# First projection of an attention and FFN layer in blocks of 2, 4 and 10 k-tiles, with moved transposes and another allocation order

## The chip, the cores and the metric

One core of a Trainium2 chip runs the whole layer as one program. The metric is the time of one execution in device microseconds (us), as the median of three runs: 2285.63 us for the kernel before. The profile is of one further execution on the same program.

## The reference

The reference is one encoder layer on x of 512 tokens by 2048 features in float32. Cut to what matters here:

```python
mod = c_act @ w_ada[l] + b_ada[l]                       # 2048 x 12288 weights for one vector
sh1, sc1, gt1, sh2, sc2, gt2 = split(mod, 6)
h = rms_norm(x, g_norm1[l]) * (1 + sc1) + sh1
proj = h @ w_in[l]                                      # q, k, v of 8 differential heads, latents
a_out = differential_attention(q_d, k_d, v_d, lam, rel_bias)
b_out = latent_attention(q_m, k_m, v_m)                 # 8 heads from the latents
x = x + gt1 * (concatenate([a_out, b_out]) @ w_out[l])
h2 = rms_norm(x, g_norm2[l]) * (1 + sc2) + sh2
x = x + gt2 * ((silu(h2 @ w_gate[l]) * (h2 @ w_up[l])) @ w_down[l])
```

## The kernel before

Every product is made of three matmuls on operands that are split into a high and a low part (`mm3`, lines 241 to 243): high by high, high by low, low by high. ACT makes the high part of a weight chunk (line 89), DVE or POOL the low part (line 97). PE runs its instructions in the order of the program; the instructions of the other engines are put in order by a scheduler, which follows the program's order loosely.

**First stage.** x is held as 16 tiles `xs[t][b]` of 128 x 512. The modulation's shift and scale for `nk` k-tiles of 128 features are sums over 16 rows of w_ada per partition: `ada_pair` loads 512 KB a step into one of five `araw` buffers (line 330) and DVE adds it, times c, to an accumulator (lines 334 and 336). `ada_columns` turns a finished accumulator into columns with small matmuls (line 347). `modulation` scales x by rstd, transposes each k-tile on PE (line 398), and ACT and DVE make from it the high and low parts `hh` and `hl` (lines 400 to 402). One k-tile of one head is 12 matmuls of 384 columns.

The k-tiles come in the blocks (0, 2), (2, 2), (4, 4), (8, 4), (12, 4), given as first tile and count. For each block the first five heads (`FIRST = 5`) run `head_block`, and the partial result goes to SBUF (`raw_in`; line 506 copies, line 508 adds). In the last block only head 0 runs there; the last four tiles of heads 1 to 4 are the first part of the filling. While a block runs, `run` steps two generators as PE's estimated progress goes on: the sums for the block after next, and the modulation of the next block. What is left of them is emptied at the block's end. Ahead of the first block stand the loads in the order of `LOADS` (`a` a step of the sums, `x` a tile of x, `w` the first weight chunk).

**Attention.** `projections` is one long generator of matmuls: the rest of heads 1 to 4, all 16 k-tiles of heads 5 to 7, the latents (`cq`, `ckv`, `latents`), then four pairs of latent heads and parts of the output projection. `Filler` runs so many us of it, by its own prices, at each F of a written order of steps: s scores, t transposes of probabilities, v values, n norm of the next head, o its operands, e `finish` of the head before. `finish` transposes on PE four tiles `z`, the last of which POOL scales at the end of the head before (lines 739 to 742, 748). `fill.until` runs the generator in one piece until a condition holds. Behind the first pair the generator yields nothing until the latent heads start.

**FFN.** Gate and up run first plainly for two column groups, then in units of seven block products with operands `comb` and `wh`, `wl` (lines 1253 to 1255). The down projection runs in six parts over the hidden features with the same `project` as the output projection. Its stationary tiles are `ax` (part 0: `act0`), its moving tiles the weights `hi` and `lo` of pool `fw`. In the program before, pool `fd` holds per partition 16 tiles `sums` of 2048 bytes, `gt2` of 8192 bytes, `pad` of 32 bytes, then 32 tiles `ax` of 2048 bytes and four `x1r`. `ax` starts at byte 126,944 of a partition, the weights `hi` of the down projection at 44,480. In the output projection the stationary `mh` tiles start at 108,512 and multiples of 2048 behind it, the moving `hi` at 212,960. In the units the moving `comb` starts at 85,984, the stationary `wh` at 44,480.

Of the kernel before, what the change touches and what calls it, by code (L numbers as in the profile page):

```python
# [18 lines left out]
P = 128  # L19
# [18 lines left out]
FIRST = 5  # L38
NEAR = 0.2
LOADS = "aaaxxxxaxxxxaxxxxaxxxxwaa"  # L40
BLOCKS = ((0, 2), (2, 2), (4, 4), (8, 4), (12, 4))
# [157 lines left out]
def hybrid_layer(ctx, tc, a, out):  # L199
# [182 lines left out]
    sums1 = {k0: [] for k0, _ in BLOCKS}  # L382

    def modulation_sums(k0, nk):
        yield from ada_pair(raws0, accs0, 1, 0, k0, nk, sums1[k0])

    def modulation(k0, nk):
        for b in range(1, 4):
            if k0 <= 4 * b - 2 < k0 + nk:
                with tc.issue_after(last_hh[0]):  # L390
                    for t in range(NT):
                        act.activation(xs[t][b], xs[t][b], AF.Copy, scale=rstd1[:, t:t + 1])
        ada_columns(sums1[k0], k0, nk, G1, SH1, C_G1, C_BSC1, C_BSH1)
        yield None
        for kc in range(k0, k0 + nk):
            ps = bank(spare[0], "ps_x")
            for t in range(NT):
                pe.transpose(ps[:, tsl(t)], xs[t][kc // 4][:, tsl(kc % 4)], ident)
            xt, hh, hl = slot("xt", F32), slot("hh"), slot("hl")
            act.activation(xt, ps, AF.Identity, scale=G1[:, kc:kc + 1], bias=SH1[:, kc:kc + 1])  # L400
            last_hh[0] = act.copy(out=hh, in_=xt).ins
            dve.tensor_tensor(out=hl, in0=xt, in1=f(hh), op=ALU.subtract)  # L402
            hT[kc] = (hh, hl)
            yield None

    first = modulation_sums(*BLOCKS[0])
    i = 0
    for kind in LOADS:
        if kind == "a":
            next(first)  # L410
        elif kind == "w":
            W.split(0)
        else:
            t, b = divmod(i, 4)
            sp.dma_start(out=xs[t][b], in_=x[t * P:(t + 1) * P, b * 512:(b + 1) * 512])
            i += 1
# [39 lines left out]
    for t in range(NT):  # L456
        if t % 2:
            act.activation(xs[t][0], xs[t][0], AF.Copy, scale=rstd1[:, t:t + 1])
        else:
            dve.tensor_scalar(out=xs[t][0], in0=xs[t][0], scalar1=rstd1[:, t:t + 1], scalar2=None, op0=ALU.mult)  # L460

# [85 lines left out]
    for gen in (first, modulation(*BLOCKS[0]), modulation_sums(*BLOCKS[1])):  # L547
        for _ in gen:
            pass
    def run(gen, total, at, start, end):  # L550

        n = total * min(1.0, max(0.0, (at - start) / (end - start)))
        while gen[1] < n:
            gen[1] += 1
            next(gen[0], None)

    for i, (k0, nk) in enumerate(BLOCKS):
        final = i + 1 == len(BLOCKS)
        ahead = [modulation_sums(*BLOCKS[i + 2]) if i + 2 < len(BLOCKS) else iter(()), 0]
        near = [iter(()) if final else modulation(*BLOCKS[i + 1]), 0]  # L560
        heads = range(1 if final else FIRST)
        for h in heads:
            tag = next_tag()
            spare[0] = "tmp" if tag == "acc" else "acc"
            for j, _ in enumerate(head_block(h, k0, nk, tag)):
                at = (h + j / nk) / len(heads)
                run(ahead, 16, at, 0.0, 0.9)
                run(near, 7, at, NEAR, 0.95)
        for gen in (ahead[0], near[0]):
            for _ in gen:  # L570
                pass
# [818 lines left out]
    side = gate2()  # L1390
    pads.append(fd[1].tile([P, 8], F32, name="pad"))
# [3 lines left out]
    for i, n in enumerate(PARTS):  # L1395
        for b in range(4):
# [4 lines left out]
            if b == 0 and i + 1 < n_parts:  # L1401
# [40 lines left out]
DIFF_STEPS = "s0 F e s1 n F t0 F s2 v0 F t1 F s3 v1 F t2 F o0 v2 t3 F o1 v3 F"  # L1442
# [45 lines left out]
```

## Time and profile before

| | before |
|---|---|
| median of three runs | 2285.63 us (2285.3 to 2287.18) |
| the profiled execution | 2284.71 us |
| its span in the profile | 2282.9 us |
| mean granted clock | 0.989 |
| PE busy | 2194.7 us of the span |
| DVE busy | 1646.3 us of the span |
| DMA | 344.99 MB, mean 151 GB/s |

The span runs from the first to the last instruction. A busy PE isn't a PE at its peak: matmuls overlap in the records, so the distance between their starts tells the rate. A granted clock of 1.00 is 2.4 GHz, of 0.5 it is 1.2 GHz, and numbers between are means over a stretch.

### The profile page before, as it was taken

The numbers are of one execution on the slowest core, as the hardware profiler recorded it, in microseconds if no ns is written. First come the engines' busy times: TensorE is split into PE (matmuls) and PEld (weight loads), VectorE is DVE, ScalarE is ACT, GpSimd is POOL, SyncE is SP. The second block draws the span as 40 slices with busy tenths as digits, with TensorE's granted clock in tenths as the row PEclk, the third lists the DMA queues.
The fourth block names the chain that finished last, engine by engine and source line by source line (L and its number), as shares of the span: only waits on it lengthen the run. The fifth ranks groups of instructions, "written<-read, shape, count | busy, mean of one in ns | idle before, by whom it ended". The sixth has DMA issues, their size and how long they took to land.

```text
span 2282.9 us, 35317 instructions
## 1 busy us (share of the span) xinstructions
PE 2194.7 (96%) x13878; PEld 2004.6 (88%) x13878; DVE 1646.3 (72%) x2360; ACT 945.1 (41%) x1569; POOL 263.0 (12%) x408
## 2 busy tenths in 40 slices
PE   3899999998989999999999999999999999999999
PEld 2799989997778787899999999999999888888887
DVE  5987787868988686857777777777777676343654
ACT  4423555557555334534444444444444522221221
POOL 0002533436544000000000000000000000000000
PEclk9999999999999999999999999999999999999999
DMA  9975355432433685423333333333333786332442
GB/s 297 322 233 145 90 155 157 131 92 88 162 120 121 214 283 186 135 83 124 121 130 121 121 130 110 122 121 121 112 129 121 253 282 202 101 121 92 157 139 101
DMA packets 270825, 344.99 MB, mean 151 GB/s; under 512 B 15005, under 2 KB 171142, under 8 KB 270530
## 3 DMA queue, kind: packets, MB, share of 16 engines
q1 hardware_dynamic: 267864, 338.18, 45.8%
q10 hardware_dynamic: 2794, 4.55, 0.6%
q8 instruction: 108, 1.77, 0.3%
q14 instruction: 59, 0.48, 0.1%
HBM read 322.71 MB, written 19.96 MB: 150 GB/s over the span
## 4 chain that ended last, share of the span: by engine, by line
PE 68%; DVE 3%; DMA 2%; issue 1%; ACT 0%; POOL 0%; SPq 0%; DVEq 0%; ACTq 0%; POOLq 0%
PE ps_d L243 7%; PE ps_d L242 7%; PE ps_d L241 7%; PE ps_X L1253 5%; PE ps_X L1254 5%; PE ps_X L1255 5%; PE ps_W L1253 3%; PE ps_W L1255 3%; PE ps_W L1254 3%; PE ps_o L241 2%; PE ps_o L243 2%; PE ps_o L242 2%; PE ps_Y L1255 2%; PE ps_Z L1255 2%; PE ps_Z L1253 2%; PE ps_Y L1253 2%
## 5 line engine op out<-in xcount | busy, mean ns | idle before, releaser
L89 ACT CAST hi<-raw 128x1024 fp32r<-128x1024 f32 (+2 forms) x228 | 221.2, 971 | 508.2 <-PE ps_d L242 303.1
L97 DVE TENSOR_TENSOR lo<-raw,hi 128x1024 fp32r<-128x1024 f32 (+2 forms) x215 | 242.7, 1130 | 234.3 <-ACT hi L89 232.4
L1236 ACT CAST wh<-wr 128x1024 fp32r<-128x1024 f32 x160 | 168.6, 1054 | 242.5 <-PE ps_X L1254 68.2
L1254 PE MATMUL ps_X<-comb,wh 128*128 128x256 f32 x960 | 267.9, 279 | 0.0
L1253 PE MATMUL ps_X<-comb,wh 128*128 128x256 f32 x960 | 267.9, 279 | 0.0
L1255 PE MATMUL ps_X<-comb,wl 128*128 128x256 f32 x960 | 267.9, 279 | 0.0
L241 PE MATMUL ps_d<-hi,ax 128*128 128x512 f32 x640 | 253.1, 396 | 0.0
L242 PE MATMUL ps_d<-hi,ax 128*128 128x512 f32 x640 | 253.1, 395 | 0.0
L243 PE MATMUL ps_d<-lo,ax 128*128 128x512 f32 x640 | 253.1, 395 | 0.0
L1219 DVE TENSOR_TENSOR wl<-wr,wh 128x1024 fp32r<-128x1024 f32 x160 | 195.7, 1223 | 73.6 <-ACT wh L1236 73.5
L243 PE MATMUL ps_in<-lo,hh 128*128 128x384 f32 (+2 forms) x704 | 233.1, 331 | 9.8 <-DVE lo L97 9.8
L241 PE MATMUL ps_in<-hi,hh 128*128 128x384 f32 (+2 forms) x704 | 237.9, 338 | 3.4 <-ACT hi L89 2.6
L242 PE MATMUL ps_in<-hi,hl 128*128 128x384 f32 (+2 forms) x704 | 232.3, 330 | 0.8 <-DVE hl L402 0.7
L1236 ACT CAST wh<-wt 128x1024 fp32r<-128x1024 f32 x120 | 126.2, 1051 | 195.6 <-PE ps_X L1254 118.8
L1219 DVE TENSOR_TENSOR wl<-wt,wh 128x1024 fp32r<-128x1024 f32 x120 | 146.8, 1224 | 78.5 <-ACT wh L1236 78.5
L1254 PEld LDWEIGHTS ps_X<-comb,wh 128*128 128x128 f32 x960 | 180.4, 188 | 0.0
L1253 PEld LDWEIGHTS ps_X<-comb,wh 128*128 128x128 f32 x960 | 180.4, 188 | 0.0
L1255 PEld LDWEIGHTS ps_X<-comb,wl 128*128 128x128 f32 x960 | 180.4, 188 | 0.0
L1253 PE MATMUL ps_W<-comb,wh 128*128 128x256 f32 x640 | 179.2, 280 | 0.9 <-DVE cu L1264 0.9
L1254 PE MATMUL ps_W<-comb,wh 128*128 128x256 f32 x640 | 178.6, 279 | 0.0
L1255 PE MATMUL ps_W<-comb,wl 128*128 128x256 f32 x640 | 178.6, 279 | 0.0
L243 PEld LDWEIGHTS ps_in<-lo,hh 128*128 128x128 f32 x704 | 136.5, 194 | 11.4 <-DVE lo L97 11.4
(320 smaller groups left out, 5328.1 us busy)
## 6 DMA issues: line engine op xcount, KB each, us to landing
raw<-in_w_down_dram SPq DMA_DIRECT2D x88, 512.0 KB
araw<-in_w_ada_dram SPq DMA_DIRECT2D x80, 512.0 KB
wr<-in_w_gate_dram SPq DMA_DIRECT2D x40, 1024.0 KB
wr<-in_w_up_dram SPq DMA_DIRECT2D x40, 1024.0 KB
ada<-in_w_ada_dram SPq DMA_DIRECT2D x128, 256.0 KB
raw<-in_w_in_dram SPq DMA_DIRECT2D x128, 192.0 KB
raw<-in_w_out_dram SPq DMA_DIRECT2D x32, 512.0 KB
x<-in_w_ada_dram SPq DMA_DIRECT2D x64, 256.0 KB
```

The source lines that it names most:

```text
L89: nc.scalar.copy(out=hi[:, :n], in_=raw[:, :n])
L97: e.tensor_tensor(out=lo[:, :n], in0=raw[:, :n], in1=hi[:, :n].bitcast(F32), op=ALU.subtract)
L241: pe.matmul(o, ah, bh, start=start, stop=False)
L242: pe.matmul(o, al, bh, start=False, stop=False)
L243: pe.matmul(o, ah, bl, start=False, stop=stop)
L1219: dve.tensor_tensor(out=out, in0=x, in1=y, op=ALU.subtract)
L1236: act.copy(out=hi, in_=src)
L1253: pe.matmul(ps[bk], wh[:, k], c[:, 0], start=first and k == 0, stop=False, skip_group_check=True)
L1254: pe.matmul(ps[bk], wh[:, k], c[:, 1], start=False, stop=False, skip_group_check=True)
L1255: pe.matmul(ps[bk], wl[:, k], c[:, 0], start=False, stop=k == 7, skip_group_check=True)
```

## The change

The words that come with it: first stage in blocks of 2, 4 and 10 k-tiles with six heads, x loaded first; five heads' last ten k-tiles as filling; also pad order and later transposes. `FIRST` is not touched by the diff.

x is loaded ahead of all else. The first two k-tiles get their sums, transposes and evacuation before any head. The sums and modulations of the other k-tiles are paced by windows of PE's estimated us (`MODULATE`), and at a block's end those that start below the end of the next block are emptied. In the step order of the differential heads `e` moves back by two fillings. In the down projection the first tile pair of part 1 is loaded ahead of the allocation of `pad`. A scratch area of SBUF gets 1024 bytes per partition; before, it had 16,384.

```diff
+MODULATE = ((0, 2, (0, 0), (0, 0)), (2, 4, (0.0, 21.0), (21.0, 25.0)), (6, 4, (23.0, 40.0), (41.0, 48.0)),
+            (10, 4, (40.0, 58.0), (59.0, 66.0)), (14, 2, (58.0, 67.0), (67.5, 74.0)))
-BLOCKS = ((0, 2), (2, 2), (4, 4), (8, 4), (12, 4))
+BLOCKS = ((0, 2), (2, 4), (6, 10))
...
+    def evacuate(kc, ps, both):
+        xt, hh, hl = slot("xt", F32), slot("hh"), slot("hl")
+        if both:
+            last_hh[0] = act.activation(hh, ps, AF.Identity, scale=G1[:, kc:kc + 1], bias=SH1[:, kc:kc + 1]).ins
+            dve.tensor_scalar(out=xt, in0=ps, scalar1=G1[:, kc:kc + 1], scalar2=SH1[:, kc:kc + 1], op0=ALU.mult,
+                              op1=ALU.add)
+        else:
+            act.activation(xt, ps, AF.Identity, scale=G1[:, kc:kc + 1], bias=SH1[:, kc:kc + 1])
+            last_hh[0] = act.copy(out=hh, in_=xt).ins
+        dve.tensor_tensor(out=hl, in0=xt, in1=f(hh), op=ALU.subtract)
+        hT[kc] = (hh, hl)
...
+    for i in range(16):
+        t, b = divmod(i, 4)
+        sp.dma_start(out=xs[t][b], in_=x[t * P:(t + 1) * P, b * 512:(b + 1) * 512])
...
+    k0, nk, _, _ = MODULATE[0]
+    for _ in modulation_sums(k0, nk):
+        pass
+    spare[0] = "acc"
+    psx = [turned(kc) for kc in range(k0, k0 + nk)]
+    spare[0] = "tmp"
+    W.split(0)
+    W.load(1)
+    W.load(2)
+    ada_columns(sums1[k0], k0, nk, G1, SH1, C_G1, C_BSC1, C_BSH1)
+    for i in range(nk):
+        evacuate(k0 + i, psx[i], True)
+    W.split(1)
...
+    def run(g, at):
+        gen, n, done, (start, end) = g
+        due = n * min(1.0, max(0.0, (at - start) / (end - start)))
+        while g[2] < due:
+            g[2] += 1
+            next(gen, None)
+
+    at = 0.0
+    side1 = [[paced(modulation_sums(k0, nk), 4 * nk + 1, s), paced(modulation(k0, nk), nk + 1, m)]
+             for k0, nk, s, m in MODULATE[1:]]
     for i, (k0, nk) in enumerate(BLOCKS):
         final = i + 1 == len(BLOCKS)
+        for h in range(1 if final else FIRST):
             tag = next_tag()
             spare[0] = "tmp" if tag == "acc" else "acc"
+            for us in head_block(h, k0, nk, tag):
+                for pair in side1:
+                    for g in pair:
+                        run(g, at)
+                at += us * 1.07
+        while not final and side1 and MODULATE[-len(side1)][0] < BLOCKS[i + 1][0] + BLOCKS[i + 1][1]:
+            for g in side1.pop(0):
+                for _ in g[0]:
+                    pass
         if i == 1:
             load_small()
...
     side = gate2()
+    more = load_acts(1)
+    next(more)
     pads.append(fd[1].tile([P, 8], F32, name="pad"))
...
-            if b == 0 and i + 1 < n_parts:
+            if b == 0 and 0 < i < n_parts - 1:
                 more = load_acts(i + 1)
...
-DIFF_STEPS = "s0 F e s1 n F t0 F s2 v0 F t1 F s3 v1 F t2 F o0 v2 t3 F o1 v3 F"
+DIFF_STEPS = "s0 F s1 n F t0 F e s2 v0 F t1 F s3 v1 F t2 F o0 v2 t3 F o1 v3 F"
...
-    nc = _bacc.Bacc("TRN2", target_bir_lowering=False, num_devices=1)
+    nc = _bacc.Bacc("TRN2", target_bir_lowering=False, num_devices=1, dynamic_dma_scratch_size=1024)
```

## Rows read from the trace of the kernel before

**Rows 1.** The page, first part: busy us, share of the span, instructions of each engine.

```profile
PE 2194.7 (96%) x13878; PEld 2004.6 (88%) x13878; DVE 1646.3 (72%) x2360; ACT 945.1 (41%) x1569; POOL 263.0 (12%) x408
```

**Rows 2.** Windows: length, then busy us (instructions) by engine; granted clock, DMA share, GB/s.

```profile
core 0: us, PE busy (x) PEld busy (x) DVE busy (x) ACT busy (x) POOL busy (x), PEclk, DMA share, GB/s
33.00:157.70 124.70, 107.09 (x565) 103.11 (x566) 114.42 (x150) 49.52 (x78) 0.00 (x0) 0.93 0.95 304
0.00:20.00 20.00, 0.31 (x1) 0.18 (x1) 6.24 (x12) 6.85 (x15) 0.20 (x4) 1.00 0.76 237
20.00:40.00 20.00, 3.27 (x16) 3.27 (x16) 9.50 (x18) 9.95 (x26) 1.21 (x2) 1.00 1.08 353
100.00:120.00 20.00, 13.80 (x54) 13.49 (x55) 19.46 (x25) 4.96 (x7) 0.00 (x0) 0.74 0.93 302
```

**Rows 3.** PE: one group up to 215.4 us; timeline starts: 50 matmuls, and the stage's last.

```profile
L241 PE MATMUL ps_in<-hi,hh 128*128 128x384 f32 x256 | 91.8, 359 | 3.2 <-ACT hi L89 2.6 <-ACT hh L401 0.7
...
199.84 0.33 PE L241 MATMUL ps_in<-hi,hh 128*128 128x384 f32 x1
...
208.33 0.33 PE L242 MATMUL ps_in<-hi,hl 128*128 128x384 f32 x1
...
215.26 0.33 PE L243 MATMUL ps_in<-lo,hh 128*128 128x384 f32 x1
```

**Rows 4.** Timeline of PE up to the first head's first matmul: start, length, instructions.

```profile
36.73 1.87 PE L347 MATMUL ps_ada<-ones,adaacc 128*128 128x1 f32 x8 [32.14 <-DVE adaacc L336]
38.46 1.95 PE L398 MATMUL ps_x<-ident,xs 128*128 128x128 f32 x8
41.07 0.69 PE L241 MATMUL ps_in<-hi,hh 128*128 128x384 f32 x1 [0.66 <-ACT hh L401]
```

**Rows 5.** DVE groups up to 200 us (busy us, mean ns, idle before); timeline: the last sum.

```profile
L336 DVE SCALAR_TENSOR_TENSOR adaacc<-araw,c_col,adaacc 128x1024 f32<-128x1024 f32 x45 | 57.6, 1279 | 0.4 <-DMA araw<-in_w_ada_dram 0.2
L97 DVE TENSOR_TENSOR lo<-raw,hi 128x768 fp32r<-128x768 f32 x30 | 28.5, 954 | 10.3 <-ACT hi L89 9.7
L508 DVE TENSOR_TENSOR raw_in<-raw_in,ps_in 128x384 f32<-128x384 f32 x48 | 25.7, 549 | 4.8 <-PE ps_in L243 4.7
L336 DVE SCALAR_TENSOR_TENSOR adaacc<-araw,c_col,adaacc 128x512 f32<-128x512 f32 x30 | 22.5, 751 | 12.5 <-DMA araw<-in_w_ada_dram 11.7
L402 DVE TENSOR_TENSOR hl<-xt,hh 128x512 fp32r<-128x512 f32 x16 | 11.0, 687 | 2.4 <-ACT hh L401 2.3
...
156.38 1.27 DVE L336 SCALAR_TENSOR_TENSOR adaacc<-araw,c_col,adaacc 128x1024 f32<-128x1024 f32 x1
```

**Rows 6.** DMA issues up to 210 us: count and KB each.

```profile
araw<-in_w_ada_dram SPq DMA_DIRECT2D x48, 512.0 KB
...
araw<-in_w_ada_dram SPq DMA_DIRECT2D x32, 256.0 KB
xs<-in_x_dram SPq DMA_DIRECT2D x16, 256.0 KB
```

**Rows 7.** PE's waits, 217 to 520 us (us, times, longest); a window as in rows 2.

```profile
PE ps_zT L748 <- POOL z L742: 9.3, 4, 5.6
...
320.00:340.00 20.00, 14.41 (x74) 13.40 (x74) 13.08 (x31) 6.39 (x14) 9.34 (x13) 0.91 0.46 130
```

**Rows 8.** Windows around the change from differential to latent heads.

```profile
510.00:530.00 20.00, 17.72 (x113) 15.77 (x112) 12.17 (x24) 17.62 (x60) 11.61 (x32) 0.91 0.26 84
540.00:570.00 30.00, 24.99 (x140) 21.67 (x139) 26.47 (x65) 18.55 (x51) 19.56 (x39) 0.94 0.33 115
```

**Rows 9.** Timeline of PE, first and last of 51 (down), 52 (out), 51 (units) matmuls.

```profile
1999.92 0.40 PE L242 MATMUL ps_d<-hi,ax 128*128 128x512 f32 x1
...
2011.58 0.40 PE L241 MATMUL ps_d<-hi,ax 128*128 128x512 f32 x1
...
783.62 0.39 PE L242 MATMUL ps_o<-hi,ml 128*128 128x512 f32 x1
...
795.18 0.39 PE L242 MATMUL ps_o<-hi,ml 128*128 128x512 f32 x1
...
1059.76 0.28 PE L1255 MATMUL ps_Z<-comb,wl 128*128 128x256 f32 x1
...
1065.60 0.28 PE L1254 MATMUL ps_W<-comb,wh 128*128 128x256 f32 x1
```

More of the change, by code (lines that the diff above doesn't have):

```diff
@@ L38 @@
 FIRST = 5
-NEAR = 0.2
-LOADS = "aaaxxxxaxxxxaxxxxaxxxxwaa"
-BLOCKS = ((0, 2), (2, 2), (4, 4), (8, 4), (12, 4))
+MODULATE = ((0, 2, (0, 0), (0, 0)), (2, 4, (0.0, 21.0), (21.0, 25.0)), (6, 4, (23.0, 40.0), (41.0, 48.0)),
+            (10, 4, (40.0, 58.0), (59.0, 66.0)), (14, 2, (58.0, 67.0), (67.5, 74.0)))
+BLOCKS = ((0, 2), (2, 4), (6, 10))
 PARTS = (2, 4, 4, 4, 4, 4)
@@ L381, in hybrid_layer, with turned @@
     last_hh = [None]
-    sums1 = {k0: [] for k0, _ in BLOCKS}
+    sums1 = {m[0]: [] for m in MODULATE}
     def modulation_sums(k0, nk):
         yield from ada_pair(raws0, accs0, 1, 0, k0, nk, sums1[k0])
+    def evacuate(kc, ps, both):
[9 more added lines that the diff above has]
+        hT[kc] = (hh, hl)
+    def turned(kc):
+        ps = bank(spare[0], "ps_x")
+        for t in range(NT):
+            pe.transpose(ps[:, tsl(t)], xs[t][kc // 4][:, tsl(kc % 4)], ident)
+        return ps
     def modulation(k0, nk):
@@ L395, in modulation @@
         for kc in range(k0, k0 + nk):
[L396 to L403, printed above, removed]
-            yield None
[L406 to L416, printed above, removed]
+            evacuate(kc, turned(kc), False)
+            yield None
+    for i in range(16):
+        t, b = divmod(i, 4)
+        sp.dma_start(out=xs[t][b], in_=x[t * P:(t + 1) * P, b * 512:(b + 1) * 512])
     ps = bank("tmp", "ps_small")
@@ L545, in bias_strips, with paced @@
             sp.dma_start(out=vecd[:, i * 512:(i + 1) * 512], in_=vec[0:H, :])
[L547 to L555, printed above, removed]
+    def paced(gen, n, span):
+        return [gen, n, 0, span]
+    def run(g, at):
[7 more added lines that the diff above has]
+             for k0, nk, s, m in MODULATE[1:]]
     for i, (k0, nk) in enumerate(BLOCKS):
         final = i + 1 == len(BLOCKS)
[L559 to L562, printed above, removed]
+        for h in range(1 if final else FIRST):
             tag = next_tag()
             spare[0] = "tmp" if tag == "acc" else "acc"
[L565 to L571, printed above, removed]
+            for us in head_block(h, k0, nk, tag):
[7 more added lines that the diff above has]
+                    pass
         if i == 1:
```

## The prediction

> **What bounds the kernel now.** I read the page first: PE is busy 2194.7 of 2282.9 us [rows 1], so nearly all that can be won lies where PE waits, and in how far apart its matmuls start. Windows show where it waits. Until the first matmul of a head at 41.07 us it does almost nothing [rows 4], and from there to 120 us it runs in pieces, with a granted clock of 0.74 between 100 and 120 us [rows 2]; that is a part of the time at 1.2 instead of 2.4 GHz. At full clock the 384-column matmuls of this stage start 8.49 us / 49 = 0.1733 us apart [rows 3]. The 3 x 256 of them up to head 0's last block [rows 3] are 768 x 0.1733 = 133.1 us of work, and the last one starts at 215.3 us [rows 3]: some 82 us of this stage went elsewhere, 41 of them before the first matmul.
>
> What PE waits for there is DVE's sums of w_ada. From 33 us to 157.7 us, where the last sum begins at 156.38 us [rows 5], DVE is busy 114.42 of 124.70 us, while the DMA share is 0.95 at 304 GB/s [rows 2]. DVE is the nearer bound and DMA close behind. After that PE is full, but for two kinds of holes: 9.3 us of waits of the transposes of finish() for POOL's z, the longest 5.6 us [rows 7], and the change from the differential heads to the latent heads, where PE is busy 17.72 of 20 us and 24.99 of 30 us [rows 8].
>
> The last view is the timeline of steady stretches. In the down projection 512-column matmuls start 11.66 us / 50 = 0.2332 us apart; in the output projection, which is the same function with the same shapes, 11.56 us / 51 = 0.2267 us; in the gate and up units 256-column ones 5.84 us / 50 = 0.1168 us [rows 9]. Nothing waits in any of them.
>
> **The change, part by part.** I sum against the profiled execution's 2284.7 us; the median is 0.9 us above it.
>
> *First stage.* The words speak of six heads and of five as filling; the diff leaves FIRST at 5, so five heads run blocks 0 and 1, head 0 alone runs the ten-tile block, and four heads' ten tiles become filling. PE's work up to head 0's last block falls from 64 to 5 x 6 + 10 = 40 head-tiles of 12 matmuls, 480 x 0.1733 = 83.2 us; the other 49.9 us go into the filling, which between 217 and 520 us loses only the waits of [rows 7], so they count there at full rate. The first stage gains if head 0 ends before 215.4 - 133.1 + 83.2 = 165.5 us.
>
> The start gets quicker. x is 16 loads of 256 KB [rows 6], 4.2 MB; all now stand ahead of w_ada on SP's queue, so at 353 GB/s [rows 2] they land by about 3 + 12 + 2 = 17 us, the squares and rstd end near 20 us, and the two turned tiles wait in PSUM. The 4.2 MB of the first sums follow by 29 us; 16 sums of 0.75 us [rows 5] keep step. From there the old path took 4.3 us to a matmul, with ada columns and transposes one after the other [rows 4]; without the transposes about 3. First matmul near 33 us instead of 41.
>
> But this is not where head 0's end is set. The rule that empties the pending generators compares with the end of the next block. After block 1 that end is 16, so the sums and modulations of all ten tiles stand in PE's order ahead of the ten-tile block. Blocks 0 and 1 advance the paced clock by 30 x 2.09 = 62.7 us, and the last generators' spans reach to 74, so they are emptied, not finished, there. PE cannot start head 0's block before DVE's last sum. DVE's work up to it, from 17.7 us on: 32 sums of 0.75 and 48 of 1.28 us, 17 lo of 0.95 (15 chunks and two ahead), 20 adds of 0.55 and 16 hl of 0.69, two evacuations more [rows 5]: 24 + 61 + 16 + 11 + 11 + 1 = 124 us. At 100% that ends at 142 us, at the 92% of [rows 2] at 152 us. DMA has 4.2 (x) + 33.5 (w_ada) [rows 6] + 5.9 + 1 (15 weight chunks of 393 KB and two or three ahead) = 45 MB to bring, at 304 to 353 GB/s 130 to 151 us. I take 146 us. Then four ada columns and eight transposes (2.9 us at the rate of [rows 4]), some 1.5 us of low clock after the wait, and 20.8 us of matmuls: head 0 ends at 171 us, 5.5 late against 165.5. **First stage: +5 us** (-2 with 139 us, +15 with 155 us). PE's own work ahead of the last sum, 33 + 62.4 + about 10 us, ends long before 146 and is covered; if DVE were quicker, it would be late next at about 110 us.
>
> Small loads: use_small and the bias strips now follow head 0's last block, since block 2 is now the final one. They are a few PE and DVE instructions that the strip's DMA follows, and 20 us of start filling cover it; without that cover some 3 us. SP's queue: the paced w_ada loads stand ahead of weight loads, which may wait for a raw buffer up to five chunks ahead of PE; at about 7 us a chunk that is slack of 35 us, so I cost it at nothing. The smaller scratch and `dve` splits of the moved chunks cost nothing that a row shows; these splits of 0.95 us are 20 in 83 us of filling, beside a DVE with room.
>
> *finish() later.* Step e moves behind s1, n and two more fillings. Between the last values of a head and its transposes there now lie four fillings of 2.9 us, not two, and s1 and t0: about 14 us instead of 7. The longest wait was 5.6 us beyond 7, so all four vanish: 9.3 us, and after the longest the stretch of 20 us had a clock of 0.91 [rows 7], about 1.5 us more. What is late next is the softmax that these waits had hidden, at t0, which keeps its two fillings. **-10 us** (bounds -12.5 and -5).
>
> *More filling.* The budget of fillings to head 7's first operand step is 20.8 + 182 + 20 = 223 us. Needed for the first latent pair: by the paced prices 208 us before, 208 + 46.9 = 255 now. So 32 us, the end of the latent projections, latents() and the first pair, run in one piece in front of that step. PE is full in the projections, but latents' POOL chain and the pair's K chain stand bare; in the old stretches of [rows 8] 2.3 + 5 us and some low clock were lost on the same chains and on missing filling. I take **+3 us** (-5 to +8).
>
> *Pad order.* pad is 32 bytes per partition. Allocated behind the first tile pair of `ax` it no longer shifts `ax`, whose addresses become multiples of 64 bytes like those of the down weights; today they are 32 off. In the output projection stationary and moving tiles are both 32 off and go at 0.2267 us; in the down projection they differ and go at 0.2332 us; in the units they differ too [rows 9]. If equal offsets are what counts, the 1920 matmuls of parts 1 to 5 gain 1920 x 0.0065 = 12.5 us. The bounds: nothing, if the place has no effect; 6 us, if each tile counts by itself; a loss of as much as 12.5 us isn't excluded by a row. The units speak half against equality: 0.1168 x 2 is 0.2336 per 512 columns, just the slow rate, but a fixed cost per matmul would make the fast one 0.120 there. I take **-12.5**, since the two 512-column stages run one function and differ in addresses alone. The Trainium skill, "TensorE: Matmul & The Clock Gate", section "Back-to-back issue gap", makes the gap of a warm matmul a function of its columns and the clock alone (N / 2.4 + 2.5 ns); the two 512-column stretches disagree with it, and by it this part would be 0 and the sum 2282.7 us.
>
> One tile of part 1 is loaded earlier: one load, one cast, one subtraction beside a full PE, nothing.
>
> Sum: 2284.7 + 5 - 10 + 3 - 12.5 = 2270.2, about **2270 us**.
>
> **Rivals.** (a) The address has no effect, or half: 2282.7 or 2276.5 us, up to 2290 if it hurts. For it: the units. Against it: one function at two rates. The section of the Trainium skill named above would have it so.
> (b) Slower: the last sum comes late. Its place is the emptying ahead of the ten-tile block, where every us of DVE's last sum is a us of PE. With the other parts as forecast (-19.5), the kernel is slower by over 0.2% once head 0 ends 24.1 us past 165.5, that is with the last sum at 165 us or later. At 270 GB/s 45 MB take 167 us, the sum ends near 170, and the time is 2295 us. For it: the first 20 us brought 237 GB/s, DVE and DMA now need each other at every step. Against it: 304 GB/s held for 125 us with more weights among them [rows 2].
> (c) The change does what its words say, six heads: 12.5 us more of PE work under the same wait for about 4 us more of DVE and DMA, 2262 us. Or head 7's holes close with the filling, about 2262 as well. Against the first: FIRST in the diff.
>
> **How the numbers follow.** 0.2% is about what a measurement of this kernel can tell from no change: 4.6 us, so faster is below 2281.1, slower above 2290.2. Forecast 0.55 (2257 to 2281); (a) 0.27, of which 0.14 faster, 0.11 within, 0.02 slower; (b) 0.10, of which 0.02 within, 0.08 slower; (c) 0.08, faster. The forecast's edge gives 0.01 to "within". Faster 0.54 + 0.14 + 0.08 = 0.76; same 0.01 + 0.11 + 0.02 = 0.14; slower 0.10. The range for 8 in 10 reaches from 2257 (sum at 141 us, finish -11, pad full) to 2286, which takes in (a) with a first stage 3 us worse.
>
> **What would show it.** Right: first matmul near 33 us; DVE's last sum at 141 to 151 us, PE waiting for it just ahead of the ten-tile block; no wait of ps_zT for POOL up to 500 us; 24 matmuls of the down projection in 5.44 us, not 5.60. Wrong: the same 0.2332 us there (then (a)); a last sum after 160 us (then (b)); new holes of over 10 us ahead of the first latent head.

## The result, and the profile after

The changed kernel takes 2313.15 us (median of 4 runs, 2311.44 to 2314.76) beside 2286.40 us for the kernel before in the same session: a ratio of 1.0117, 95% interval 1.0100 to 1.0135. That is 1.2% slower, where 2270 us was forecast and the range ended at 2286. The profiled execution has a span of 2310.2 us, 27.3 us more than before.

**Where the 27.3 us are.** The first thing to read is a timeline of PE at the same milestones in both kernels: the first scores of head 0, the first and last matmul of the gate and up units. Of the kernel before:

```profile
240.59 0.39 PE L699 MATMUL ps_s<-k,q 128*128 128x512 f32 x1
...
997.27 0.28 PE L1253 MATMUL ps_X<-comb,wh 128*128 128x256 f32 x1
...
1783.29 0.27 PE L1255 MATMUL ps_W<-comb,wl 128*128 128x256 f32 x1
```

The same three of the kernel after:

```profile
219.00 0.39 PE L720 MATMUL ps_s<-k,q 128*128 128x512 f32 x1
...
1034.19 0.28 PE L1274 MATMUL ps_X<-comb,wh 128*128 128x256 f32 x1
...
1823.22 0.28 PE L1276 MATMUL ps_W<-comb,wl 128*128 128x256 f32 x1
```

The first scores come 21.6 us earlier. But 49.9 us of work had been put off into the filling by then, so the stage lost 28.3 us. From the first scores to the units it takes 815.2 instead of 756.7 us, 58.5 more, of which the put-off work is 49.9: a further 8.6 lost. The units take 789.0 instead of 786.0 us; in the profiles of the experiments in which their code and the offsets of their tiles are the same, they take 784.8 to 792.2, so this says nothing of the change. What follows, the down projection, takes 487.0 instead of 499.6: 12.6 won. The sum is 28.3 + 8.6 + 3.0 - 12.6 = 27.3.

**The first stage.** Windows of the kernel after; columns as in [rows 2]:

```profile
33.00:159.40 126.40, 92.42 (x464) 88.50 (x464) 105.02 (x131) 47.88 (x75) 0.00 (x0) 0.84 0.90 290
...
60.00:80.00 20.00, 12.88 (x67) 12.27 (x67) 12.70 (x16) 7.57 (x13) 0.00 (x0) 0.74 0.89 293
...
150.00:170.00 20.00, 10.52 (x47) 10.55 (x48) 11.79 (x24) 5.95 (x9) 0.00 (x0) 0.58 0.32 90
```

Up to its last sum DVE is busy 105.0 of 126.4 us, 83%; before it was 92% [rows 2]. The granted clock is 0.84 against 0.93: it falls to the half rate behind each long wait of PE, so in the window from 60 to 80 us (0.74), which holds a wait of 7.0 us. The timeline of PE shows the first head matmul and the two ends:

```profile
34.06 1.86 PE L348 MATMUL ps_ada<-ones,adaacc 128*128 128x1 f32 x8 [9.91 <-DVE adaacc L337]
37.24 0.69 PE L242 MATMUL ps_in<-hi,hh 128*128 128x384 f32 x1 [1.32 <-ACT hh L391]
...
159.48 1.84 PE L348 MATMUL ps_ada<-ones,adaacc 128*128 128x1 f32 x8 [11.52 <-DVE adaacc L337]
161.18 1.95 PE L403 MATMUL ps_x<-ident,xs 128*128 128x128 f32 x8
...
185.41 0.34 PE L244 MATMUL ps_in<-lo,hh 128*128 128x384 f32 x1
```

PE waits 11.52 us for the last sum, exactly ahead of the ten-tile block, and head 0 ends at 185.4 us. DVE, for its part, stands still at each modulation. Its timeline, with the wait in brackets:

```profile
75.25 0.16 DVE L349 TENSOR_TENSOR G<-ps_ada,small 128x4 f32<-128x4 f32 x1 [3.73 <-PE ps_ada L348]
...
77.67 0.69 DVE L397 TENSOR_TENSOR hl<-xt,hh 128x512 fp32r<-128x512 f32 x1 [2.06 <-ACT hh L396]
...
154.65 4.68 DVE L337 SCALAR_TENSOR_TENSOR adaacc<-araw,c_col,adaacc 128x512 f32<-128x512 f32 x6
```

It waits for PE's columns, then for ACT's casts, with the next sums behind these in its queue; the last six sums run to 159.3 us. DVE's waits from 40 to 157 us (us, times, longest), first of the kernel after, then of the kernel before:

```profile
DVE G L349 <- PE ps_ada L348: 7.9, 3, 3.7
DVE lo L98 <- ACT hi L90: 5.4, 5, 2.6
DVE hl L397 <- ACT hh L396: 4.5, 2, 2.5
```

```profile
DVE G L348 <- PE ps_ada L347: 4.2, 2, 3.5
DVE hl L402 <- ACT hh L401: 1.5, 2, 1.2
DVE lo L97 <- ACT hi L89: 1.2, 2, 0.7
```

These are 17.8 us instead of 6.9. For its loads DVE waits 0.7 us in that stretch.

**A hole at 211 us.** The largest group of PE's waits between 190 and 240 us (us, times, longest):

```profile
PE ps_in L244 <- DVE lo L98: 4.6, 1, 4.6
```

The longest single wait but one of SP's queue between 20 and 220 us, and the timeline of POOL:

```profile
SPq L298 <- POOL ada L297: 8.1, 1, 8.1
```

```profile
193.87 5.33 POOL L687 TENSOR_TENSOR qd<-raw_in,rs 128x256 f32<-128x256 f32 x8
199.15 0.52 POOL L297 MEMSET ada<- 128x512 f32 x1
```

SP waits for a memset that stands behind head 0's norm on POOL; the loads of the first gate and of the weights queue behind it. In the kernel before the same memset had run at 188 us, ahead of that norm.

**The heads.** The waits of ps_zT for POOL [rows 7] are gone: between 240 and 500 us the largest group of PE's waits is

```profile
PE ps_in L242 <- ACT raw_in L535: 1.7, 2, 1.1
```

The change to the latent heads, on the other hand, has become worse than in [rows 8]. PE's waits from 510 to 600 us, and the window:

```profile
PE ps_kT L897 <- POOL kn L878: 11.8, 4, 9.8
PE ps_l L802 <- POOL raw_in L812: 5.9, 1, 5.9
PE ps_zT L769 <- POOL z L763: 1.8, 1, 1.8
```

```profile
550.00:600.00 50.00, 30.32 (x156) 26.38 (x155) 17.08 (x34) 24.00 (x70) 34.49 (x70) 0.80 0.28 95
```

**The down projection.** Two starts 25 matmuls apart:

```profile
2049.79 0.39 PE L242 MATMUL ps_d<-hi,ax 128*128 128x512 f32 x1
...
2055.46 0.39 PE L243 MATMUL ps_d<-hi,ax 128*128 128x512 f32 x1
```

5.67 us / 25 = 0.2268 us instead of 0.2332 [rows 9].

### The profile page after: what moved, and what is told of

Same layout as the page of the kernel before. It is cut to its first block, busy times and chain, and to the rows that moved or that the text cites. A ratio compares the mean times of both kernels' runs of the same rounds, so it can differ in the third digit from the quotient of the medians.

```text
span 2310.2 us, 35265 instructions
## 1 busy us (share of the span) xinstructions
PE 2188.9 (95%) x13878; PEld 2010.0 (87%) x13878; DVE 1622.5 (70%) x2312; ACT 946.4 (41%) x1567; POOL 279.6 (12%) x418
## 4 chain that ended last, share of the span: by engine, by line
PE 65%; DVE 4%; DMA 3%; issue 1%; POOL 0%; ACT 0%; SPq 0%; DVEq 0%; ACTq 0%; POOLq 0%
PE ps_d L242 7%; PE ps_d L244 7%; PE ps_d L243 7%; PE ps_X L1274 5%; PE ps_X L1276 5%; PE ps_X L1275 5%; PE ps_W L1274 3%; PE ps_W L1276 3%; PE ps_W L1275 3%; PE ps_o L242 2%; PE ps_o L244 2%; PE ps_o L243 2%; PE ps_Z L1276 1%; PE ps_Z L1274 1%; PE ps_Y L1276 1%; PE ps_Y L1274 1%
## 5 line engine op out<-in xcount | busy, mean ns | idle before, releaser
L98 DVE TENSOR_TENSOR lo<-raw,hi 128x1024 fp32r<-128x1024 f32 (+2 forms) x205 | 232.6, 1135 | 232.6 <-ACT hi L90 232.2
L243 PE MATMUL ps_d<-hi,ax 128*128 128x512 f32 x640 | 249.0, 389 | 0.0
L242 PE MATMUL ps_d<-hi,ax 128*128 128x512 f32 x640 | 249.0, 389 | 0.0
```

The source lines that it names most:

```text
L98: e.tensor_tensor(out=lo[:, :n], in0=raw[:, :n], in1=hi[:, :n].bitcast(F32), op=ALU.subtract)
L242: pe.matmul(o, ah, bh, start=start, stop=False)
L243: pe.matmul(o, al, bh, start=False, stop=False)
```

## The experiments

A difference of under 3 us between two medians is not told apart here. The kernel after was timed in one session only, the kernel before in all of them, with medians from 2285.53 to 2288.19 us; so where a run is set beside the kernel after, the difference is good to some 3 us. What was expected of each run, with a theory and a rival, was written before it ran.

### The address of `ax`

The first try, on the kernel before:

```diff
-    pads.append(fd[1].tile([P, 8], F32, name="pad"))
+    pads.append(fd[1].tile([P, 16], F32, name="pad"))
```

> The kernel before with one edit: the pad ahead of the `ax` tiles is 64 bytes per partition instead of 32, so that `ax` lies a multiple of 64 bytes in, as in the kernel after, while the order of loads and of everything else stays. Theory (the address alone sets the spacing): 24 matmuls of the down projection take 5.44 us instead of 5.60, 1920 x 0.0065 = 12.5 us less, about 2274 us. Rival (it was the order of loads, or the earlier first tile): still 5.60 us, and 2286 us, the time of the kernel before.

2288.51 us beside 2288.19; 24 matmuls in 5.60 us. This tested nothing of the address: the pool grows from its far end, so `ax` kept its place and the tiles ahead of the pad moved by 32 bytes, which made no difference that can be told. The second try moves `ax` and keeps the order of the loads:

```diff
-    pads.append(fd[1].tile([P, 8], F32, name="pad"))
...
                     next(more, None)
+                if not pads:
+                    pads.append(fd[1].tile([P, 8], F32, name="pad"))
```

> The kernel before with one edit: the pad of 32 bytes is allocated behind `ax` and its neighbours, after the first load of part 1, so that `ax` lies at a multiple of 64 bytes as in the kernel after, while loads and their order stay as they were. (In the run with the pad of 64 bytes `ax` had kept its address, since this pool grows from its far end and only what stands ahead of the pad moved.) Theory (the address of `ax` sets the spacing): 24 matmuls of the down projection in 5.44 us instead of 5.60, 12.5 us less, 2274 us. Rival (the order of the loads, or something else of the change, sets it): 5.60 us and 2286 us.

2273.79 us beside 2285.83, ratio 0.9946 (0.9925 to 0.9966). The timeline of this kernel's down projection, 25 matmuls apart:

```profile
2049.76 0.39 PE L243 MATMUL ps_d<-lo,ax 128*128 128x512 f32 x1
...
2055.43 0.39 PE L241 MATMUL ps_d<-hi,ax 128*128 128x512 f32 x1
```

Again 5.67 us. Address alone, 12.0 us: the theory holds. The converse, on the kernel after, shifts the other side:

```diff
+    shift = const.tile([P, 8], F32, name="shift")
     ident = const.tile([P, P], F32, name="ident")
```

> The kernel after with one edit: an unused tile of 32 bytes per partition ahead of the constants moves every tile on that side by 32 bytes, the stationary tiles of the units and of the down projection among them, so that in the down projection stationary and moving tiles lie 32 bytes apart again (`ax` at a multiple of 64, the weights 32 off), and in the units they now agree (both 32 off). Theory (equal offsets within 64 bytes are what counts): the down projection goes back to 5.60 us for 24 matmuls, 12.5 us more; the units change too, by 0.120 instead of 0.1168 us a matmul, 6720 x 0.0032 = 21 us more if the rate of the other 256-column matmuls holds there, or not at all; 2325 to 2347. Rival (only the moving tile's address counts): 5.44 us stay, the units stay, 2313.

2343.17 us, ratio to the kernel before 1.0244 (1.0223 to 1.0266), 30 us over the kernel after. The expectation calls the shifted tiles stationary in both places; in the down projection they are the moving ones (`hi`, `lo`), in the units the stationary ones (`wh`, `wl`). Timelines of this kernel: the units, 50 matmuls apart, then the down projection, 25 apart:

```profile
1399.73 0.28 PE L1277 MATMUL ps_X<-comb,wl 128*128 128x256 f32 x1
...
1405.73 0.28 PE L1276 MATMUL ps_X<-comb,wh 128*128 128x256 f32 x1
...
2099.79 0.39 PE L242 MATMUL ps_d<-hi,ax 128*128 128x512 f32 x1
...
2105.62 0.40 PE L243 MATMUL ps_d<-hi,ax 128*128 128x512 f32 x1
```

The down projection is back at 5.83 / 25 = 0.2332 us, and the units, whose offsets now agree, went from 0.1168 to 6.00 / 50 = 0.1200 us. In the units only the stationary tile moved, as `ax` alone did in the run before; so neither tile's own address counts, but how the two stand to each other. All eighteen profiles agree: 24 matmuls on `ax` take 5.44 us in the thirteen where the offsets of `ax` and its weights agree, and 5.60 us in the five where they are 32 bytes apart (medians over the projection).

### finish() alone

```diff
-DIFF_STEPS = "s0 F e s1 n F t0 F s2 v0 F t1 F s3 v1 F t2 F o0 v2 t3 F o1 v3 F"
+DIFF_STEPS = "s0 F s1 n F t0 F e s2 v0 F t1 F s3 v1 F t2 F o0 v2 t3 F o1 v3 F"
```

> The kernel before with one edit: the step e of the order of a head's steps stands behind the second filling after n, as in the kernel after. Theory (the waits of ps_zT for POOL vanish and little is late in their place): the 9.3 us of waits between 280 and 380 us are gone, with 1.5 us of low clock, some 10 us less, about 2276 us. Rival (the softmax and the splits, which those waits hid, are late next): holes of 3 to 6 us stand elsewhere between 240 and 520 us, and it gains 4 to 6 us, 2280 to 2282.

2284.95 us beside 2288.19, ratio 0.9982 (0.9970 to 0.9995): 3 us, less than even the rival gave. PE's waits of this run, 240 to 500 us:

```profile
PE ps_z L732 <- DVE aTl L608: 4.6, 2, 3.2
PE ps_z L729 <- DVE aTl L608: 1.0, 1, 1.0
```

The waits of ps_zT are gone, and the values wait for DVE's split of the turned probabilities instead, the stretch that the old waits had covered.

### The ten-tile block undone

```diff
-MODULATE = ((0, 2, (0, 0), (0, 0)), (2, 4, (0.0, 21.0), (21.0, 25.0)), (6, 4, (23.0, 40.0), (41.0, 48.0)),
-            (10, 4, (40.0, 58.0), (59.0, 66.0)), (14, 2, (58.0, 67.0), (67.5, 74.0)))
-BLOCKS = ((0, 2), (2, 4), (6, 10))
+MODULATE = ((0, 2, (0, 0), (0, 0)), (2, 2, (0.0, 4.0), (4.2, 19.8)), (4, 4, (0.0, 18.8), (25.1, 40.7)),
+            (8, 4, (20.9, 39.7), (50.2, 81.5)), (12, 4, (41.8, 79.4), (92.0, 123.3)))
+BLOCKS = ((0, 2), (2, 2), (4, 4), (8, 4), (12, 4))
```

> The kernel after with one part undone: the blocks of the kernel before, (0, 2), (2, 2), (4, 4), (8, 4), (12, 4), for five heads, and the spans of MODULATE set to them as the old code spread them; x first, early transposes, step e and the pad stay. The filling is then that of before too. Theory (with ten k-tiles put off PE has too little to do ahead of DVE's last sum, and the put-off work stands bare behind it): PE's waits between 60 and 165 us fall below 12 us in all, the hole at 550 to 600 us goes back to that of before, and 35 to 45 us are won, 2268 to 2278. Rival (the paced generators, x first or the early transposes cost it): 2295 or more.

2271.89 us beside 2285.53, ratio 0.9943 (0.9923 to 0.9963): 41 us under the kernel after, as the theory had it. Its PE waits from 60 to 165 us, and its window:

```profile
PE ps_in L244 <- DVE lo L98: 10.1, 4, 4.1
PE ps_in L242 <- ACT hi L90: 0.8, 1, 0.8
```

```profile
33.00:159.40 126.40, 104.78 (x553) 100.55 (x554) 112.55 (x147) 47.89 (x75) 0.00 (x0) 0.92 0.92 296
```

DVE's last sum still ends at 159.8 us here, but no column matmul waits for it: PE has head-tiles to run. So the last sum's time is not what the blocks changed; it is what stands ahead of it and behind it. The hole at 211 us and the wait of ps_kT are gone as well.

The profile is of the slowest of this run's four executions and 35.6 us shorter than that of the kernel after. With 49.9 us more of work ahead of them, the first scores come only 24.3 us later (243.3): 25.6 us are won there. From the scores to the units it takes 757.4 us instead of 815.2 less the put-off 49.9: 7.9 us won. The units give 2.0.

### Why it costs: the emptying, the pace, the heads, the buffers

Less emptying, on the kernel after:

```diff
-        while not final and side1 and MODULATE[-len(side1)][0] < BLOCKS[i + 1][0] + BLOCKS[i + 1][1]:
+        while not final and side1 and MODULATE[-len(side1)][0] < BLOCKS[i + 1][0] + 1:
```

> The kernel after with one edit: a block's end empties only the generators of the first k-tiles of the next block, so (10, 4) and (14, 2) stay paced inside head 0's ten-tile block. Theory (what is dear is that PE's order puts the last modulation ahead of head 0's whole last block): PE starts that block while DVE still sums, its first four to eight tiles cover the wait of 11.5 us and the half clock after it, head 0 ends near 168 us instead of 185, and the time falls by 14 to 20 us, to 2293 to 2299. Rival (DVE's own chain is what is late, and the wait only moves to k-tile 14 inside the block): head 0 ends near 180 us, 2306 to 2311.

2306.76 us, 6 us under the kernel after. Head 0's last matmul starts at 180.2 us and the last wait falls from 11.5 to 5.4 us: the rival.

Six heads, as the words of the change have it:

```diff
-FIRST = 5
+FIRST = 6
```

> The kernel after with one edit: FIRST = 6, so six heads run blocks 0 and 1, as the words of the change say, and the spans of MODULATE end inside block 1 (36 x 2.09 = 75 us). Theory (PE lacks work ahead of DVE's last sum, and the spans were sized for six heads, so that with five a block's end empties what is not yet due): the holes ahead of the block ends at 72 and 159 us shrink, head 5's 6 k-tiles, 12.5 us of PE work, fill them, and the time falls by 10 to 16 us, to 2297 to 2303. Rival (the sums are paced by PE's own work, so that six heads make the last sum later by as much as they fill): last sum at 168 us or later, under 5 us less, 2308 to 2313.

2324.29 us, 11 us slower: both missed. With 12.5 us more of PE's work the first scores come only 7.1 us later (226.1), so the stage itself gains 5; the last sum ends at 162.4. But from there to the units it takes 819.3 instead of 815.2 us, with 12.5 us less to do, and between 300 and 430 us PE has new waits:

```profile
PE ps_row L365 <- ACT ada L361: 7.1, 1, 7.1
PE ps_in L242 <- ACT raw_in L535: 3.9, 1, 3.9
```

What makes the gate's row late there stays open.

A quicker pace, the same emptying:

```diff
-MODULATE = ((0, 2, (0, 0), (0, 0)), (2, 4, (0.0, 21.0), (21.0, 25.0)), (6, 4, (23.0, 40.0), (41.0, 48.0)),
-            (10, 4, (40.0, 58.0), (59.0, 66.0)), (14, 2, (58.0, 67.0), (67.5, 74.0)))
+MODULATE = ((0, 2, (0, 0), (0, 0)), (2, 4, (0.0, 16.0), (16.5, 20.0)), (6, 4, (17.0, 31.0), (32.0, 38.0)),
+            (10, 4, (31.0, 45.0), (46.0, 53.0)), (14, 2, (45.0, 52.0), (53.0, 59.0)))
```

> The kernel after with one edit: the spans of MODULATE are cut by a fifth to a quarter, so that the last modulation is due at 59 us of the paced clock and five heads' blocks 0 and 1 (62.7 us) finish all of them without emptying. Theory (DVE stands still because the sums are handed to it at PE's pace and then in lumps): DVE is busy over 92% from 40 us to the last sum, which ends near 150 us instead of 159, head 0 ends near 175 us, and the time falls by 7 to 12 us, to 2301 to 2306. Rival (the last sum is set by the order PE, columns, DVE, ACT at each modulation, whatever the pace): the last sum within 3 us of 159 us, 2309 to 2314.

2312.48 us, no gain, the rival's time, though the last sum moved by more than the rival's 3 us. It ends at 155.1 us, 4 us earlier, but PE's waits for adaacc grew from 22.8 to

```profile
PE ps_ada L348 <- DVE adaacc L337: 27.4, 4, 8.4
```

since the columns moved forward with the sums. Head 0's last matmul starts at 186.8.

More buffers, on the kernel after:

```diff
-        return st[1].tile([P, 1024], F32, tag="araw", bufs=5, name="araw")
+        return st[1].tile([P, 1024], F32, tag="araw", bufs=9, name="araw")
```

> The kernel after with one edit: nine buffers for the loads of w_ada instead of five. Theory (SP's queue, which stands waiting for a free buffer, lets DVE run dry or late): DVE's last sum comes at 152 us or earlier, PE's waits for adaacc between 60 and 165 us fall from 22.8 us to under 15, and the time falls by 6 to 10 us, to 2303 to 2307. Rival (DVE stands still because its own order makes it wait for PE's columns and ACT's casts, whatever has landed): last sum within 3 us of 159 us, 2310 to 2315.

2309.87 us, last sum at 159.7 us, PE's waits for adaacc 23.3 us: the rival. Loads are not what DVE waits for.

Sums early and modulations late, with the relaxed emptying of above:

```diff
-MODULATE = ((0, 2, (0, 0), (0, 0)), (2, 4, (0.0, 21.0), (21.0, 25.0)), (6, 4, (23.0, 40.0), (41.0, 48.0)),
-            (10, 4, (40.0, 58.0), (59.0, 66.0)), (14, 2, (58.0, 67.0), (67.5, 74.0)))
+MODULATE = ((0, 2, (0, 0), (0, 0)), (2, 4, (0.0, 16.0), (18.0, 20.5)), (6, 4, (17.0, 32.0), (50.0, 60.0)),
+            (10, 4, (32.0, 50.0), (62.0, 68.0)), (14, 2, (50.0, 58.0), (70.0, 76.0)))
```

> The kernel after with the relaxed emptying and other spans of MODULATE: the sums of all k-tiles are handed out early (the last ones due at 58 us of the paced clock), the modulations as late as the ten-tile block allows (k-tile 10 at 68, k-tile 14 at 76). Theory (the order is what costs: PE and DVE wait for each other at each modulation): PE's waits for adaacc between 60 and 165 us fall under 10 us, DVE's last sum comes near 150 us, and the time falls by 15 to 20 us, to 2293 to 2298. Rival (PE simply has too little to do ahead of the sums, so that the wait only moves to another place): head 0 ends at 178 us or later, 2303 or more.

2301.21 us, 12 us under the kernel after, between the two expectations. PE's waits, 60 to 165 us:

```profile
PE ps_in L244 <- DVE lo L98: 8.2, 8, 1.8
PE ps_in L242 <- ACT hi L90: 7.5, 6, 2.5
PE ps_ada L348 <- DVE adaacc L337: 4.7, 1, 4.7
```

The waits for adaacc fell from 22.8 to 4.7 us, so the order of sums and columns is a real part of the cost. Head 0 ends 10.6 us earlier than in the kernel after, of which the relaxed emptying alone had given 5.2. But 15.7 us of waits for weights came in their place, and head 0's last matmul starts at 174.8 us, still 9 us behind the 165.5 from which putting work off would have paid. DVE stays at 105.3 of 125 us, 84%.

### The filling, and SP's queue

```diff
-DIFF_FILL = (26.0, 26.0, 26.0, 26.0, 26.0, 26.0, 26.0, 26.3)
+DIFF_FILL = (32.0, 32.0, 32.0, 32.0, 32.0, 32.0, 32.0, 26.3)
```

> The kernel after with one edit: 32 us of filling per head instead of 26 in heads 0 to 6, so that the 47 us of filling that were added are run by head 7's first operand step instead of ahead of it in one piece. Theory: the holes between 550 and 600 us (5.9 us of waits of ps_l and 11.8 us of ps_kT for POOL, and low clock behind them) close to about those of the kernel before, 9 to 14 us less, 2299 to 2304. Rival (the chains of latents and of the pair on POOL are bare wherever they run, or the filling then runs out in the latent heads): under 4 us less, 2309 to 2313.

2305.23 us, 8 us under the kernel after, a little short of the theory's range. From the first scores (219.2) to the units (1031.5) it is 812.3 instead of 815.2 us, 3 us less; but with the filling untouched this stretch took 812.4 to 816.3 us in the other profiles with these blocks, five heads and the early gate, so where the gain lies is not told. PE's waits from 510 to 600 us:

```profile
PE ps_kT L897 <- POOL kn L878: 8.0, 4, 6.0
...
PE ps_l L802 <- POOL raw_in L812: 0.7, 3, 0.2
```

The first hole closed, the second shrank by a third. So, still more, with the relaxed emptying (its line stands above):

```diff
-DIFF_FILL = (26.0, 26.0, 26.0, 26.0, 26.0, 26.0, 26.0, 26.3)
+DIFF_FILL = (36.0, 36.0, 36.0, 36.0, 36.0, 36.0, 36.0, 26.3)
```

> The kernel after with two edits together: the relaxed emptying, which gave 7 us, and 36 us of filling a head instead of 32 (32 gave 10 us and closed the wait of ps_l but not that of ps_kT). Theory (what was left of the hole at 582 us is filling that is still missing ahead of head 7's first operand step): the wait of ps_kT for POOL falls under 2 us, together 22 to 27 us less than 2313, 2286 to 2291. Rival (the pair's K chain on POOL is bare wherever the first pair stands): the wait stays at 5 us or more, 2294 to 2298.

2300.66 us, worse than both expectations. PE's waits from 510 to 600 us:

```profile
PE ps_aT L743 <- DVE pm L734: 5.8, 1, 5.8
PE ps_zT L769 <- POOL z L763: 4.6, 2, 2.8
PE ps_l L802 <- POOL raw_in L812: 3.8, 3, 2.6
```

The wait of ps_kT vanished, as the theory said; now the filling is used up before head 7's last steps, which stand bare. From first scores (212.3) to units (1023.7) it is 811.4 us: the hole moves, it does not go.

The first gate later, on the kernel after:

```diff
-GATE_EARLY = True
+GATE_EARLY = False
```

> The kernel after with one switch changed: the first gate's loads and sums come after the first latent pair has started instead of with the first head (GATE_EARLY off). Theory (SP's queue waits 8.1 us for POOL's memset, with weight loads behind it): the wait of ps_in for lo at 211 us is gone, the first scores come 4 to 6 us earlier than 219 us, and the time is 2 to 6 us less unless the latent heads give it back. Rival (the weight loads were late anyway): a wait of 3 us or more stays between 200 and 220 us, 2312 or more.

2370.53 us. PE has no wait at all between 190 and 240 us, and the first scores come at 210.6 us, 8.4 us earlier: 7.1 of them in the hole itself, where the same 33 matmuls start within 5.7 instead of 12.7 us, and 1.3 ahead of head 0's end. That the early gate, as it stands here, makes the hole is shown. That it does so through SP's wait for the memset is read from the waits, since this run takes the gate's loads and sums away too; for it speaks the run with the old blocks, which keeps the early gate: there the memset runs at 192.4 us, ahead of the norm, SP doesn't wait for POOL, and the hole is gone. But with this switch the gate lies among the latent heads, where PE waits from 810 to 880 us:

```profile
PE ps_ada L348 <- DVE ada L309: 53.3, 3, 24.7
```

### Parts on the kernel before, and the best version

x ahead of w_ada:

```diff
-LOADS = "aaaxxxxaxxxxaxxxxaxxxxwaa"
+LOADS = "xxxxxxxxxxxxxxxxaaaaaawaa"
```

> The kernel before with one part of the change: all 16 loads of x ahead of the loads of w_ada on SP's queue (the order string only; blocks, pacing and transposes stay). Theory (it brings squares and rstd forward but takes the first 12 us of DMA from DVE's sums): the first head matmul comes within 2 us of 41 us, DVE's last sum some 2 to 4 us after 157.7 us, and the time is within 3 us of 2286. Rival (the start is worth what it brings forward): first matmul at 37 us and 3 to 5 us less in total, 2281 to 2283.

2284.33 us beside 2285.53, ratio 0.9993 (0.9980 to 1.0005): no difference that can be told. First matmul at 40.1 us; the last sum, at 156.6 us, was not later, though the theory had it 2 to 4 us later.

The pad behind `ax` (as above) and step e moved (as above), nothing else:

> The kernel before with two parts of the change: the pad behind `ax`, and step e moved. Theory (the parts stand by themselves: 12.0 us measured for the address, 3 to 4 us for step e): 2269 to 2272, faster than either kernel. Rival (the two share a cover or disturb each other): 2273 or more.

2269.66 us beside 2285.53, ratio 0.9931 (0.9914 to 0.9949). This beats both kernels. The same with nine buffers for w_ada and the small scratch:

```diff
-        return st[1].tile([P, 1024], F32, tag="araw", bufs=5, name="araw")
+        return st[1].tile([P, 1024], F32, tag="araw", bufs=9, name="araw")
...
-    nc = _bacc.Bacc("TRN2", target_bir_lowering=False, num_devices=1)
+    nc = _bacc.Bacc("TRN2", target_bir_lowering=False, num_devices=1, dynamic_dma_scratch_size=1024)
```

> The kernel before with the pad behind `ax`, step e moved, the small scratch, and nine buffers for w_ada instead of five. Theory of the buffers: PE's waits for lo and adaacc from 41 to 120 us (some 11 us in the kernel before) halve, 2262 to 2267. Rival (buffers don't matter): 2268 to 2272, as the two parts alone.

2272.28 us, ratio 0.9936 (0.9921 to 0.9952): 2.6 us more than without them, which is not told apart: the buffers don't matter here either.

## Why the prediction was wrong, step by step

**Where the miss lies.** The forecast of 2270.2 us is for a profiled execution, which took 2312.0: 41.8 us more. The first stage took 23.3 of them (+28.3 for +5), the heads 15.6 (+8.6 for the -10 and +3 of finish() and filling), the units 3.0, which say nothing. The pad met its term.

**The start: 33 us forecast, 37.24 measured.** The columns begin at 34.06, still waiting for DVE's sum: 15 of the 16 first sums run in one piece from 22.2 to 34.0 us, behind rstd and the scaling of x, where the prediction let them keep step with the loads, to 29. It wouldn't have mattered: x first by itself is worth nothing that can be told.

**The last sum: "I take 146 us".** This is the step that failed first, and the largest. It came at 159.3 us, outside even its bounds of 139 to 155. DVE's work was not counted too small: 124 us from 17.7 us on, and from there to the last sum DVE is busy 116.7 us. What failed is its waiting. 146 us leaves DVE 4 us to stand still, and even the 92% of [rows 2], read from another order of work, would leave 11; it stood still for 24.9 of 141.6 us. It waited 9.9 us for PE's columns, 9.9 for ACT's casts and 0.7 for loads, with the next sums behind these waits in its queue. The run with sums early and modulations late took 18 us off PE's waits for the sums and 10.6 off head 0's end; the run with more buffers shows that loads are not the cause. Head 0 ended at 185.4 instead of 171 us, 14.4 of the 41.8, so the stage stood 20 us over its bar of 165.5, not 5. Why the last sum ends as late with the old blocks isn't settled; DVE has more to do there by then (125.3 us of 142.1).

**What the bar hid.** That PE's own work "ends long before 146 and is covered" was true and was the trouble: PE had too little to do. In the run with the old blocks the last sum is as late (159.8) and costs nothing, because PE has matmuls to run beside it: from 33 to 159.4 us it runs 553 instead of 464. Rival (b) had place and sign; its point, 165 us, was never reached. The kernel became slower at 159.3 because the other parts did not bring the 19.5 us that (b) took from them.

**SP's queue: costed at nothing.** It cost a wait of 4.6 us at 211 us and, with the low clock behind the wait, 7.1 us up to the first scores. The slack of five weight chunks was argued for waits on buffers; the wait was for POOL, whose memset had come to stand behind head 0's norm. Together with the 20 us above and some 2 us of small matmuls that now follow head 0, this makes up the 28.3 us of the stage, within 1 us.

**finish(): -10 forecast, -3 measured alone.** The four waits vanished as forecast. What is late next was named ("the softmax that these waits had hidden") and given 0: it took back most, as waits of ps_z for DVE.

**More filling: +3 forecast.** Between first scores and units 8.6 us were lost, and the run with the old blocks, which keeps step e, wins 7.9 of them back; so some 8 us belong here, at the end of the bounds of -5 to +8. The place was right (POOL's chains ahead of head 7's operands, 17.7 us of waits), the size was not. Spreading the filling brought the time down by 8 us, but its profile doesn't show that this was won here. What holds the rest, when no single wait is large, stays open.

**The pad: -12.5 forecast, -12.6 in the trace, -12.0 alone.** Right, in cause and size. The Trainium skill, "TensorE: Matmul & The Clock Gate", section "Back-to-back issue gap", gives N / 2.4 + 2.5 ns for an isolated warm matmul, some 216 ns at 512 columns, and some 131 ns for 512 columns in a stream of weight loads and matmuls, neither with a term for an address; by it the run with the pad behind `ax` would have shown no difference. The measurement decides: the same matmuls on the same data took 0.2268 or 0.2332 us by 32 bytes of address, both longer than either figure.

## What to carry to other kernels

Work that can be put off is also cover: before it is moved out of a stage that waits for another engine, ask what PE will do during that wait, and whether the stage that receives it had holes to fill; here the first lost 28 us, and the second gave none of it back. A busy share read from one order of work doesn't hold for another order in which the engines wait for each other in turn. And where one function runs at two rates, compare the addresses of its two operands.

## What was not expected of the hardware

The offset of the stationary against the moving tile, within 64 bytes, works both ways. With equal offsets a matmul of 512 columns starts every 0.2268 us and one of 256 every 0.1200 us; 32 bytes apart it is 0.2332 and 0.1168 us. At the full granted clock, 2.4 GHz, these are 544, 288, 560 and 280 cycles: columns + 32 when the offsets agree, columns x 35/32 when they don't. That is a fit to four points; the two would meet near 341 columns.

Rows of the kernel before bear out the first form. In the first projection the offsets agree (all tiles `hi`, `lo`, `hh` and `hl` of it start 32 bytes past a multiple of 64, the first `hi` at 212,960 and the first `hh` at 112,608). Its 384-column matmuls start every 0.1733 us [rows 3], which is 416 cycles, 384 + 32; by the other form it would be 420. Its 256-column ones, 33 apart:

```profile
433.28 0.28 PE L243 MATMUL ps_in<-lo,hh 128*128 128x256 f32 x1
...
437.24 0.28 PE L243 MATMUL ps_in<-lo,hh 128*128 128x256 f32 x1
```

3.96 us / 33 = 0.1200 us, as in the shifted units. The second form rests on 256 and 512 columns alone, and no distances but 0 and 32 bytes were seen. In two profiles, of the pad of 64 bytes and of the relaxed emptying, the units went at 0.1177 instead of 0.1167 us with the same offsets; why stays open.

So in this kernel the pad is right for the down projection, and the 32 bytes that remain between `comb` and the units' weights are right for the units: making them agree cost some 18 us (806.9 instead of 789.0 us in the profiles).
